# Conditioning vectors of layer 1 made on VectorE in the feed-forward of layer 0 instead of on TensorE in the mixer of layer 1

## The chip, the cores and the metric

The kernel runs on one core of a Trainium2 chip. The metric is device microseconds of one execution; the time of a kernel is the median of several. All times in the text are microseconds (us) unless marked ns. TensorE is PE in the rows (PEld: its weight loads), VectorE is DVE, ScalarE is ACT, and SP is the engine that issues the DMAs.

## The reference, cut to what matters

A batch of one sequence with 256 tokens of width 1024 goes through a first block of two layers and a second block of two layers, all in float32. The change lies in the first block alone. There every layer takes six vectors of width 1024 from one conditioning vector c:

```
ada = silu(c) @ w_ada[l] + b_ada[l]          # 1024 -> 6 * 1024
sh1, sc1, gt1, sh2, sc2, gt2 = split(ada)    # segments 0 .. 5
u = x * (1 + sc1) + sh1                      # mixer: attention, convolution, gates, w_out -> y
x = layer_norm(alpha * x + (1 + gt1) * y)
u = x * (1 + sc2) + sh2
x = layer_norm(alpha * x + (1 + gt2) * (relu(u @ w_up) ** 2 @ w_down))
```

A segment is a product of one row with a matrix of 1024 x 1024: 4 MB of weights are read for 1024 numbers. Segments 0, 1, 3 and 4 are wanted as columns (one number per partition), the gates 2 and 5 as a row on all partitions.

## The kernel before, in words

The weights stream from DRAM once. `weight_order` lists their pieces (1 MB each) in the order of use. `fetch` loads a piece into a `raw` buffer (3 of them), ScalarE casts it to a high part `whi` and VectorE subtracts to get the low part `wlo` (4 buffers each; lines L138 and L139, two halves of 1024 columns each). A product is three TensorE passes (high x high, high x low, low x high): `ws` with the weights stationary (L160, L161, L164), `as_` with the activations stationary (L180 to L182).

TensorE runs its instructions in the order of the program. VectorE, ScalarE and SP get an order from a planner, which goes by the order of the program and by times of its own model; on the chip every engine then keeps the order it was given. Between a product and the next one stands `handover` (residual, norm, feature-major operand), whose order on TensorE, VectorE and ScalarE is written out by hand.

Side work is a generator that `track` and `tick` advance: `track(gen, steps, us)` spreads so many steps over so many us of the main stream, and `ws_pair`, `branch` and the loop of `ffn1` call `tick` with what they take. So the place of a side step in the program, and with it the place of its TensorE instructions, is set by its number.

Conditioning has two forms. On VectorE, `ada_work` takes segments as 8 items of 128 rows or columns each. Item n loads a tile of 512 KB into one of two `ada` buffers (L354; the load of item n+1 is written before the work of item n, so it takes the buffer of item n-1), and VectorE then does one pass over 128x1024: for columns a product with `c_row` and a sum (L343), for a gate a multiply-add into an accumulator `acc` (L365 for its first item, L367 for the others). Six steps after the last item of a gate follow four steps `ada_gate`: one TensorE matmul with ones (L387) that sums a quarter of `acc` over the partitions, and two VectorE operations (L388, L390). On TensorE, `ada_pe` takes a segment as four pieces of 256 columns: two loads of 512 KB (L402), eight products in four column groups (L408), a ScalarE copy (L411), and then either `ada_gate` or two products of one column each (L418) and one VectorE operation (L421).

Before the change the mixer of layer 0 makes (0,4), (0,3), (0,2) on TensorE, the feed-forward of layer 0 makes (0,5), (1,1), (1,0) on VectorE, the mixer of layer 1 makes (1,3), (1,4), (1,2) on TensorE, and the feed-forward of layer 1 makes (1,5) on VectorE. `ffn1` is a loop over c = 2 .. 18: a `ws_pair` of w_up piece c, then `Out.add` of w_down piece c-3, about 11.2 us of TensorE together, with `tick` amounting to 10.4; at c = 15 what is left of the side work is written out. Beside it runs `rel_bias`, whose last instructions are a small table written to DRAM (L571) and a DMA of 1.5 MB from DRAM to DRAM (`toep<-rv`, L573).

In the mixer VectorE also does the depthwise convolution (`conv`, L909 and L912), which `conv_ln` transposes on TensorE (L927) before the branches that use it.

Of the kernel before, what the change touches and what calls it, by code (L numbers as in the profile page):

```python
# [28 lines left out]
def _two_pi():  # L29
    """2 pi as a sum of three floats, the first two with few digits."""  # L30
    c1 = 6.28125
    c2 = np.array([2 * math.pi - c1], np.float32)
    c2 = float((c2.view(np.uint32) & np.uint32(0xFFFFF000)).view(np.float32)[0])
    return c1, c2, float(np.float32(2 * math.pi - c1 - c2))
# [4 lines left out]
# columns of the packed per-partition parameters, and of the shape constants  # L39
# [21 lines left out]
PARTS = ((0, 512), (512, 768), (768, 1024))  # of the columns at the end of a product of 1024  # L61
ADA_PE = [(0, 4), (0, 3), (0, 2), (1, 3), (1, 4), (1, 2)]


class Net:
# [36 lines left out]
    def track(self, gen, steps, us):  # L102
        """Advance gen by `steps` steps over the next `us` of the main stream."""
        t = [gen, steps / us, 0.0]
        self.tracks.append(t)
        return t
# [17 lines left out]
    def fetch(self, parts=1):  # L124
        """One packed piece of a weight: its float32 values as hi + lo, both float32r."""
        nc = self.nc
        src = self.queue.pop(0)
        cols = src.shape[-1]
        raw = self.t("raw", [P, 2048])
        for a in range(0, cols, cols // parts):  # L130
            nc.sync.dma_start(raw[:, a:a + cols // parts], src[:, a:a + cols // parts])
        hi = self.t("whi", [P, 2048], F32R)
        lo = self.t("wlo", [P, 2048], F32R)
        step = cols // 2 if cols >= 1024 else cols
        with self.later():
            for a in range(0, cols, step):
                b = a + step
                nc.scalar.copy(hi[:, a:b], raw[:, a:b])  # L138
                nc.vector.tensor_sub(lo[:, a:b], raw[:, a:b], hi[:, a:b].bitcast(F32))  # L139
        self.ready.append((hi, lo))  # L140

    def w(self, ahead=2):
        """The next piece in weight_order; the pieces after it are already on their way."""
        while self.queue and len(self.ready) < 1 + ahead:
            self.fetch()
        return self.ready.pop(0)

    def split(self, hi, lo, src):
        """src (float32) as hi + lo."""
        a = self.nc.scalar.copy(hi, src)  # L150
        return a, self.nc.vector.tensor_sub(lo, src, hi.bitcast(F32))  # L151

    def ws(self, ps, w, blk, a, ks):
        """ps[cols of the weight, tokens] = W[:, cols]^T a   (weights stationary)."""
# [11 lines left out]
    def ws_pair(self, a, w=None):  # L166
        """Two column tiles (8 k tiles each) of the next weight piece -> psum [128, 2 x 256]."""
        w = w or self.w()
        p = self.ps()
        for m in range(2):  # L170
            self.ws(p[:, m * S:(m + 1) * S], w, m * 8, a, range(8))
            self.tick(2.6)
        return p

    def as_(self, ps, w, cols, a, k, h, first, last, **grp):
        """ps[tokens of half h, cols] += a^T W   (activations stationary)."""
# [7 lines left out]
    def as_512(self, a, first=False):  # L184
        """512 columns, two pieces of four k tiles -> psum of both halves.  first: another step before the
        last products of the first half."""
# [20 lines left out]
    class Out:  # L207
        """Product with 1024 columns, pieces of two k tiles: four accumulators; the last two pieces half by
        half, in PARTS of the columns."""

# [30 lines left out]
    def rstd(self, v, w):  # L241
        """v (> 0, [128, w]) -> v ** -0.5: a guess from the exponent, two refinements."""
# [29 lines left out]
    def rstd1(self, v, mul, eps, fill=()):  # L272
        """v ([128, 1]) -> (v * mul + eps) ** -0.5; the steps of rstd, their constants gathered into one
        factor that goes into v.  fill: work for VectorE in between."""
# [18 lines left out]
    def moments(self, st, eps, fill=()):  # L293
        """st: bn_stats of the pieces of a row -> mean, rstd."""
# [4 lines left out]
    def to_fm(self, src, n, evac):  # L299
        """src: [128 tokens, n * 128] in SBUF; evac(k0, nk, psum [128, nk, 128])."""  # L300
# [15 lines left out]
    def row(self, ap, n=D, pool="b4"):  # L316
        """A row of DRAM on all partitions."""
# [12 lines left out]
    def ada_cols(self, l, seg):  # L330
        """A shift (seg 0, 3) or 1 + scale (1, 4) as columns [128, 8]."""
# [8 lines left out]
    def ada_dot(self, l, seg, k, w):  # L340
        """One tile of columns: w [128 columns, 1024]; c_row is twice SiLU(c)."""
# [4 lines left out]
    def ada_work(self, segs):  # L346
        """On VectorE."""
# [32 lines left out]
    def ada_gate(self, l, seg, n, part, bb):  # L380
        """256 columns of a gate on all partitions: part summed over the partitions, + bias, + 1."""
# [10 lines left out]
    def ada_pe(self, segs):  # L392
        """On TensorE: 256 columns at a time, four k tiles side by side in the array."""
# [30 lines left out]
    def probs(self, q, k, bias):  # L424
        """q, k: [K, 256] feature-major (q scaled); bias [128, 256].  Unnormalised softmax numerators
        e [128, 384] (block 0: 128 keys | block 1: 256 keys) and the reciprocal row sums [128, 2]."""
# [18 lines left out]
    def p_t(self, e):  # L445
        """e [128 queries, 384] -> [128 keys, 384]: keys 0 x 256 queries | keys 1 x queries of block 1."""
# [8 lines left out]
    def attend(self, qk, v, bias, y):  # L455
        """qk(h) -> q, k; v(h, j) -> [128 keys, 64]; y feature-major [128, 4, 256].  Each step: the scores of
        one head, the transposed probabilities of the one before, the output of the pair before that."""
# [32 lines left out]
    def start(self):  # L490
        """Conditioning of the first mixer tile by tile, and with each tile its share of q, k, v and the
        first two pairs of the convolution's gated input."""
# [59 lines left out]
    def rel_bias(self):  # L552
        """DRAM [head, query in block, 256]: additive bias at distance 128 + p - j, -1e30 where masked."""
# [22 lines left out]
    def rope_tables(self):  # L576
        """cos, sin of positions * inv_freq for both halves: cc = [cos | cos], ss = [-sin | sin]."""
# [32 lines left out]
    def rope_tm(self, x, cc, ss):  # L610
        """In place: x [128, heads, 2, n]; cc, ss [128, 2, n]."""
# [11 lines left out]
    def handover(self, out, ch, nxt=None):  # L623
        """out: a product, its last pieces still to come; ch: the chain of a norm on it; nxt(u): generator of
        the first product behind.  Each engine in the order given here; -> what nxt yields."""
# [36 lines left out]
    def later(self):  # L662
        """What is traced here issues behind the last handover."""
        st = ExitStack()
        for ins in self.behind:
            st.enter_context(self.tc.issue_after(ins))
        return st

    class Norm:
        """x <- LN(ALPHA x + G acc) g + b;  u <- x A + B.   rms: x <- x + 0.5 acc;  u <- RMS norm of x times g.  # L670
        y: the rows before A, B (g)."""
# [12 lines left out]
        def transposed(self, h):  # L684
            """The row tiles k = 0, 1, 4, 5 in one bank, 2, 3, 6, 7 in another."""
# [93 lines left out]
    class RMSNorm(Norm):  # L779
        """ln: x is the layer norm of ALPHA x + G acc first."""  # L780
# [135 lines left out]
    def conv_ln(self, l, cv, hc):  # L916
        """LN over the channels, SiLU."""
# [32 lines left out]
    def mixer1(self, l, u, ps):  # L950
# [21 lines left out]
        if first:  # L972
# [4 lines left out]
            ada = self.track(self.ada_pe(ADA_PE[:3]), 25, 62)  # L977
# [6 lines left out]
        else:  # L984
            keep(2, ps)
            ada = self.track(self.ada_pe(ADA_PE[3:]), 25, 80)
# [68 lines left out]
        self.finish(ada)  # L1055
# [13 lines left out]
    def ffn1(self, l, u, ps):  # L1069
        nc = self.nc  # L1070
        segs = [(0, 5), (1, 1), (1, 0)] if l == 0 else [(1, 5)]
# [56 lines left out]
    def fm_512(self, u, scale):  # L1128
        """512 columns feature-major [128, 4, 256], one piece (256 columns) per step."""
# [12 lines left out]
    def mla_norm(self, pcs, gq, n_):  # L1142
        """RMS norms of the low-rank q and kv; feature-major."""
# [23 lines left out]
    def mixer2(self, l, u, ps):  # L1167
        nc, i = self.nc, self.i
        gq = self.row(i["mla_g"][l])
        # low-rank q and kv, and the rotary key: token-major  # L1170
# [31 lines left out]
        # q of C: 64 + 32 + zeros per head  # L1202
# [18 lines left out]
        # k, v of C  # L1221
# [59 lines left out]
        # gates, then the branches  # L1281
# [33 lines left out]
    def diff(self, l, li, lam, qb, kb, vb, y):  # L1315
        """Differential attention of B, its RMS norm; y feature-major."""
# [105 lines left out]
def weight_order(i):  # L1422
    """The packed pieces of the weights in the order of their use."""
# [48 lines left out]
def _tiles(w, order, per=16):  # L1472
    """w [K, N] -> [chunks, 128, per * 128]: the 128 x 128 tiles (k, n) in the given order."""
# [18 lines left out]
def _fm(v):  # L1492
    """[..., n * 128] -> [128, ... * n]"""
# [123 lines left out]
```

## Time and profile before

| What | us |
|---|---|
| median of 3 runs | 1746.57 (1746.49 to 1747.38) |
| span of the profiled execution, first to last instruction | 1744.7 |
| median less span: what lies around the span | 1.9 |
| feed-forward of layer 0, TensorE between the handovers | about 229 to 400 |
| mixer of layer 1, first product to the next handover | about 420 to 578 |
| TensorE busy over the span | 1693.0 (97%) |

The profile is one execution. Times in its rows count from the first instruction. The own time of the profiled execution is not given beside its span; the median of the runs stands for it, 1.9 us above the span.

### The profile page before, as it was taken

The numbers are of one execution on the slowest core, as the hardware profiler recorded it, in microseconds if no ns is written. First come the engines' busy times: TensorE is split into PE (matmuls) and PEld (weight loads), VectorE is DVE, ScalarE is ACT, GpSimd is POOL, SyncE is SP. The second block draws the span as 40 slices with busy tenths as digits, with TensorE's granted clock in tenths as the row PEclk, the third lists the DMA queues.
The fourth block names the chain that finished last, engine by engine and source line by source line (L and its number), as shares of the span: only waits on it lengthen the run. The fifth ranks groups of instructions, "written<-read, shape, count | busy, mean of one in ns | idle before, by whom it ended". The sixth has DMA issues, their size and how long they took to land.

```text
span 1744.7 us, 28878 instructions
## 1 busy us (share of the span) xinstructions
PE 1693.0 (97%) x11736; PEld 1533.6 (88%) x11736; DVE 1203.8 (69%) x2281; ACT 894.8 (51%) x1550; POOL 2.6 (0%) x12
## 2 busy tenths in 40 slices
PE   6998999999999999988999999999999999999998
PEld 5887888888889899977998898999989889989997
DVE  7999887478997785468555667655675555875554
ACT  3664464355355455435566645444455666454442
POOL 0000000000000000000000000000000000000000
PEclk9999999999999999998999999999999999999999
DMA  9885568495865286635643344655454444446551
GB/s 339 339 309 188 190 228 332 168 341 187 300 233 206 97 320 217 205 130 207 209 140 130 138 156 137 239 190 191 151 210 161 147 145 145 163 158 209 183 184 47
DMA packets 59986, 347.58 MB, mean 199 GB/s; under 512 B 6558, under 2 KB 10700, under 8 KB 25676
## 3 DMA queue, kind: packets, MB, share of 16 engines
q1 hardware_dynamic: 59852, 345.73, 55.8%
q8 instruction: 92, 1.51, 0.3%
q14 instruction: 42, 0.34, 0.1%
HBM read 344.63 MB, written 2.64 MB: 199 GB/s over the span
## 4 chain that ended last, share of the span: by engine, by line
PE 89%; DVE 7%; ACT 2%; issue 1%; DMA 1%; SPq 0%; ACTq 0%; DVEq 0%
PE ps L160 16%; PE ps L161 16%; PE ps L164 16%; PE ps L181 8%; PE ps L180 8%; PE ps L182 7%; PE ps L196 3%; PE ps L202 3%; PE ps L197 3%; PE ps L430 1%; PE ps L450 1%; DVE wlo L139 1%; PE ps L306 1%; PE ps L429 1%; PE ps L408 1%
## 5 line engine op out<-in xcount | busy, mean ns | idle before, releaser
L139 DVE TENSOR_TENSOR wlo<-raw,whi 128x1024 fp32r<-128x1024 f32 (+1 forms) x534 | 630.4, 1212 | 306.1 <-ACT whi L138 304.2
L138 ACT CAST whi<-raw 128x1024 fp32r<-128x1024 f32 (+1 forms) x534 | 532.3, 1042 | 431.6 <-PE ps L161 186.2
L160 PE MATMUL ps<-s,whi 128*128 128x256 f32 x2400 | 602.6, 288 | 0.2 <-DVE s L901 0.2
L161 PE MATMUL ps<-s,whi 128*128 128x256 f32 x2400 | 590.5, 283 | 0.0
L160 PEld LDWEIGHTS ps<-s,whi 128*128 128x128 f32 x2400 | 459.8, 192 | 20.2 <-issue 16.1
L161 PEld LDWEIGHTS ps<-s,whi 128*128 128x128 f32 x2400 | 460.9, 192 | 2.4
L164 PE MATMUL ps<-s,wlo 128*128 128x256 f32 x2400 | 343.8, 284 | 1.3 <-DVE wlo L139 1.3
L164 PEld LDWEIGHTS ps<-s,wlo 128*128 128x128 f32 x2400 | 312.9, 192 | 1.5 <-DVE wlo L139 1.5
L180 PE MATMUL ps<-whi,s 128*128 128x512 f32 (+2 forms) x736 | 273.5, 372 | 12.8 <-ACT s L150 11.7
L181 PE MATMUL ps<-wlo,s 128*128 128x512 f32 (+2 forms) x736 | 273.1, 371 | 1.4 <-DVE wlo L139 1.4
L182 PE MATMUL ps<-whi,s 128*128 128x512 f32 (+2 forms) x736 | 271.8, 369 | 0.0
L180 PEld LDWEIGHTS ps<-whi,s 128*128 128x128 f32 x736 | 139.9, 190 | 34.7 <-ACT s L150 11.7
L181 PEld LDWEIGHTS ps<-wlo,s 128*128 128x128 f32 x736 | 139.9, 190 | 22.9 <-DVE wlo L139 2.5
L182 PEld LDWEIGHTS ps<-whi,s 128*128 128x128 f32 x736 | 139.6, 190 | 22.5
L196 PE MATMUL ps<-whi,s 128*128 128x512 f32 x240 | 97.9, 408 | 3.5 <-ACT s L761 3.5
L912 DVE SCALAR_TENSOR_TENSOR s<-s,dw,s 128x255 f32<-128x255 f32 (+14 forms) x240 | 96.8, 463 | 0.0
L197 PE MATMUL ps<-wlo,s 128*128 128x512 f32 x240 | 94.9, 396 | 0.0
L151 DVE TENSOR_TENSOR s<-ev,s 128x256 fp32r<-128x256 f32 (+1 forms) x72 | 39.1, 543 | 72.7 <-PE ps L181 54.0
L150 ACT CAST s<-ev 128x256 fp32r<-128x256 f32 (+1 forms) x72 | 36.1, 501 | 75.9 <-DVE ev L1392 73.5
L202 PE MATMUL ps<-whi,s 128*128 128x512 f32 x240 | 66.0, 398 | 0.0
L196 PEld LDWEIGHTS ps<-whi,s 128*128 128x128 f32 x240 | 45.8, 191 | 17.0 <-ACT s L761 5.4
L197 PEld LDWEIGHTS ps<-wlo,s 128*128 128x128 f32 x240 | 45.9, 191 | 9.1
(235 smaller groups left out, 1365.7 us busy)
## 6 DMA issues: line engine op xcount, KB each, us to landing
raw<-in_w_fgu_dram SPq DMA_DIRECT2D x44, 1024.0 KB, 4.9
raw<-in_w_up_dram SPq DMA_DIRECT2D x32, 1024.0 KB, 5.8
raw<-in_w_down_dram SPq DMA_DIRECT2D x32, 1024.0 KB, 5.1
raw<-in_w_in_dram SPq DMA_DIRECT2D x32, 1024.0 KB, 4.9
ada<-in_w_ada_p_dram SPq DMA_DIRECT2D x48, 512.0 KB, 4.6
raw<-in_w_gate_dram SPq DMA_DIRECT2D x24, 1024.0 KB, 4.8
raw<-in_w_fd_dram SPq DMA_DIRECT2D x22, 1024.0 KB, 4.8
raw<-in_w_in_b_dram SPq DMA_DIRECT2D x18, 1024.0 KB, 7.1
```

Of the source, the lines that this page charges most:

```text
L138: nc.scalar.copy(hi[:, a:b], raw[:, a:b])
L139: nc.vector.tensor_sub(lo[:, a:b], raw[:, a:b], hi[:, a:b].bitcast(F32))
L160: mm(ps, whi[:, b], ahi[:, k, :], start=j == 0, stop=False)
L161: mm(ps, whi[:, b], alo[:, k, :], start=False, stop=False)
L164: mm(ps, wlo[:, b], ahi[:, k, :], start=False, stop=j == n - 1)
L180: mm(ps, ahi[:, k, tok], whi[:, cols], start=first, stop=False, **grp)
L181: mm(ps, ahi[:, k, tok], wlo[:, cols], start=False, stop=False, **grp)
L182: mm(ps, alo[:, k, tok], whi[:, cols], start=False, stop=last, **grp)
L196: mm(p, ahi[:, k, tok], whi[:, cols], start=k == 0, stop=False)
L197: mm(p, ahi[:, k, tok], wlo[:, cols], start=False, stop=False)
L202: mm(p, alo[:, k, tok], whi[:, cols], start=False, stop=k == 7)
L912: nc.vector.scalar_tensor_tensor(cv[:, ct, d:], hp[:, ct, :S - d], wk, cv[:, ct, d:], op0=ALU.mult, op1=ALU.add)
```

## The change

`ADA_PE` keeps only the three segments of layer 0. The mixer of layer 1 runs no `ada_pe` any more. In `ffn1` of layer 0 `ada_work` gets six segments instead of three, 48 items instead of 24, with (1,2), (1,4), (1,3) behind the three of before; its track becomes 54 steps over 160 us instead of 30 over 160. The host packs fewer tiles into `w_ada_p`. The other lines of the diff take out comments.

```diff
-ADA_PE = [(0, 4), (0, 3), (0, 2), (1, 3), (1, 4), (1, 2)]
+ADA_PE = [(0, 4), (0, 3), (0, 2)]
...
-            ada = self.track(self.ada_pe(ADA_PE[:3]), 25, 62)
+            ada = self.track(self.ada_pe(ADA_PE), 25, 62)
...
             keep(2, ps)
-            ada = self.track(self.ada_pe(ADA_PE[3:]), 25, 80)
+            ada = None
...
-        self.finish(ada)
+        if ada:
+            self.finish(ada)
...
     def ffn1(self, l, u, ps):
-        segs = [(0, 5), (1, 1), (1, 0)] if l == 0 else [(1, 5)]
+        segs = [(0, 5), (1, 1), (1, 0), (1, 2), (1, 4), (1, 3)] if l == 0 else [(1, 5)]
         ada = self.track(self.ada_work(segs), 8 * len(segs) + 6, 160 if l == 0 else 80)
```

## Rows read from the trace of the kernel before

**Rows 1.** Page, part 1: busy us (share of span) x instructions.
```profile
PE 1693.0 (97%) x11736; PEld 1533.6 (88%) x11736; DVE 1203.8 (69%) x2281; ACT 894.8 (51%) x1550; POOL 2.6 (0%) x12
```

**Rows 2.** Chain of work in the mixer of layer 1: start us, us, engine, tile, line.
```profile
424.15 0.96 PE ps L164 x8
...
427.03 0.96 PE ps L164 x8
427.99 1.00 PE ps L408 x16
...
431.09 0.96 PE ps L164 x8
434.40 0.96 PE ps L164 x8
...
507.11 0.43 PE ps L387 x2
...
539.62 1.02 PE ps L927 x8
```

**Rows 3.** Stretches: length; busy PE, PEld, DVE, ACT, POOL; PEclk; DMA share; GB/s.
```profile
230.00:393.00 163.00, 161.70 (x1027) 146.47 (x1026) 115.39 (x132) 84.76 (x106) 0.00 (x0) 1.00 0.79 287
320.00:340.00 20.00, 20.00 (x122) 17.94 (x121) 2.68 (x7) 7.49 (x10) 0.00 (x0) 1.00 0.04 15
420.00:526.40 106.40, 106.40 (x834) 90.08 (x833) 100.27 (x226) 53.35 (x99) 0.00 (x0) 1.00 0.76 276
```

**Rows 4.** VectorE instructions in order of time, feed-forward of layer 0: the items.
```profile
239.57 0.75 DVE L365 TENSOR_SCALAR b<-ada,c_col 128x1024 f32<-128x1024 f32 x1
...
305.02 1.28 DVE L343 CUSTOM_DVE_ANT_0 ada<-ada,c_row,par 128x1024 f32<-128x1024 f32 x1
...
339.35 0.69 DVE L151 TENSOR_TENSOR s<-ev,s 128x512 fp32r<-128x512 f32 x1 [7.43 <-PE ps L181]
...
340.62 1.28 DVE L343 CUSTOM_DVE_ANT_0 ada<-ada,c_row,par 128x1024 f32<-128x1024 f32 x1
...
370.89 1.28 DVE L343 CUSTOM_DVE_ANT_0 ada<-ada,c_row,par 128x1024 f32<-128x1024 f32 x1
```

**Rows 5.** SP, waits of the DMA queue from 220 to 400: us, times, longest.
```profile
SPq L354 <- DVE ada L343: 59.2, 12, 28.8
SPq L354 <- DVE b L367: 17.2, 7, 3.7
```

**Rows 6.** DMA issues from 220 to 400 (median landing), then landing minimum, median, maximum.
```profile
ada<-in_w_ada_t_dram SPq DMA_DIRECT2D x16, 512.0 KB, 6.5
```
```profile
DMA to landing us min/median/max: 3.7/6.2/14.0
```

**Rows 7.** SP in order of time around the table DMA.
```profile
301.93 0.88 SPq L573 DMA_DIRECT2D toep<-rv  x1
302.93 4.40 SPq L354 DMA_DIRECT2D ada<-in_w_ada_t_dram  x1
...
309.31 0.33 SPq L354 DMA_DIRECT2D ada<-in_w_ada_t_dram  x1
```

**Rows 8.** TensorE in order of time: first gate matmul; first product of c = 14.
```profile
318.46 0.59 PE L387 MATMUL ps<-b,ones 128*128 128x256 f32 x2
```
```profile
363.73 0.28 PE L160 MATMUL ps<-s,whi 128*128 128x256 f32 x1
```

**Rows 9.** VectorE in order of time: last convolution step, first handover operation of layer 0.
```profile
525.52 0.81 DVE L912 SCALAR_TENSOR_TENSOR s<-s,dw,s 128x226 f32<-128x226 f32 x2
```
```profile
395.17 0.68 DVE L721 TENSOR_TENSOR ev<-ps,G 128x512 f32<-128x512 f32 x1
```

**Rows 10.** Stretches around TensorE's stand in the mixer of layer 0, columns as in 3.
```profile
152.00:154.00 2.00, 1.24 (x5) 1.06 (x6) 2.00 (x4) 0.00 (x0) 0.00 (x0) 0.50 0.00 0
154.00:156.00 2.00, 2.00 (x12) 2.00 (x11) 2.00 (x5) 0.00 (x0) 0.00 (x0) 0.50 0.03 8
156.00:158.00 2.00, 2.00 (x13) 1.95 (x13) 2.00 (x7) 0.00 (x0) 0.00 (x0) 0.75 0.47 66
```

## Prediction

> **What bounds the kernel now.** The page's first part comes first: TensorE is busy 97% of the span [rows 1], so work taken off it should count in full wherever nothing else comes to the fore. Next the two stages that the change touches, as stretches [rows 3]: in both TensorE is the only engine without idle time, but VectorE is close behind, 115.4 us of 163 in the feed-forward of layer 0, and 100.3 of 106.4 in the mixer of layer 1 up to the end of its convolution. So the mixer has little room under TensorE. Then the items in the feed-forward, in order of time [rows 4], and what their loads wait for [rows 5]: SP waits 76 us for VectorE to give an `ada` buffer back. That stream is held by its two buffers.
>
> **What is removed.** In the chain [rows 2] two halves of a `ws_pair` start 2.88 us apart (424.15, 427.03); with eight L408 products between them it is 4.06 (427.03 to 431.09), with L418 between them 3.31 (431.09 to 434.40). A piece of `ada_pe` thus costs TensorE 1.18 + 0.43 us; a gate's piece has L387 in place of L418, also 0.43. Twelve pieces are 12 x 1.61 = 19.3 us, all but one L387 ahead of the transposes L927 at 539.62 [rows 2], which would come 18.9 us earlier, at 520.7. They need the convolution, which VectorE ends at 526.3 [rows 9]. VectorE has 106.4 - 100.27 = 6.1 us idle up to there [rows 3]: with all of it gone the convolution ends at 520.2, as now at 526.3. So TensorE would wait at L927 between 0 and 5.6 us, or longer if work that stands behind 526 now (weights and softmax that the faster TensorE wants sooner) moves in ahead; I take 4. The mixer of layer 0 has such a wait: TensorE stands, and when it is back at 152.8 its granted clock is 0.50, the lower of its two levels (1.2 GHz), until about 157 [rows 10]; that costs 1.24 x 0.5 + 1 + 0.5 = 2.1 us. With 2 for this the mixer gives 19.3 - 4 - 2 = 13.3 us, with bounds of 10 and 19. The 24 loads of 512 KB that leave it, and the ScalarE copies, were hidden under TensorE and give nothing.
>
> **What is added to the feed-forward of layer 0.** Four gate matmuls, 4 x 0.43 = 1.7 us of TensorE. On VectorE 24 passes of at most 1.28 us [rows 4], 30.7 us, and eight small gate operations; VectorE has 163 - 115.4 = 47.6 us free [rows 3], so by the sum it fits. The 24 loads are 12.6 MB, which over 163 us add 77 GB/s to the 287 of the stretch [rows 3]; I give that no term of its own, since the two buffers hold the loads back first. The sums hide the order, and there I see the cost.
>
> The gate (1,2) is items 24 to 31. Its matmuls stand in TensorE's order at step n + 2 = 39 with n = 37 (six after item 31). The rule for the place: with 30 steps in 160 us the gate (0,5) comes at step 15, tick 80, and (80 - 5.2)/10.4 = 7.19 loops, which is the middle of the pair of c = 10; there it is, at 318.46 [rows 8]. With 54 steps, step 39 is tick 115.6, 10.61 loops, the end of c = 13. TensorE now passes that place at 363.73 [rows 8]. TensorE keeps its order, so if item 31 is not done by then, all products behind wait for it.
>
> When is item 31 done? Item 0 starts at 239.57, item 15 at 305.02 [rows 4]: 4.36 us each. Items 16 to 23 go from 340.62 to 370.89: 4.32 each. That is what two buffers allow: a load waits for the item two before, lands after 6.5 us in the median of this stage [rows 6], and the item takes 1.28; (6.5 + 1.28)/2 = 3.9, and some waits. Writing the items closer together in the program doesn't make this faster, since SP already waits for buffers. So at 305 the stream would again be near item 15.
>
> Between 305 and 340.62 there is a pause. The table DMA is issued at 301.93 [rows 7], and the two items whose loads come behind it stand in VectorE's order after L151 of c = 11 at 339.35, which waits for TensorE [rows 4]; the weights issued behind it are as late, and for 20 us the DMA engines are almost empty [rows 3]. My reading is that the planner expects that DMA to hold up the loads behind it much longer than it does. The table stays where it is, so I expect the pause again, with item 16 near 340.6. By 363.73 item 21 has started (340.62 + 5 x 4.32 = 362.2). Ten more are wanted. While TensorE stands, the weights' loads soon stop for want of buffers, and an item's load can land as fast as the quickest here, 3.7 us [rows 6]: (3.7 + 1.28)/2 = 2.5 us each. Item 31 then starts at 387.2 and ends at 388.5: TensorE waits 24.8 us, and 2.1 more go to its clock. Bounds: 43 us if the loads get no faster (340.62 + 15 x 4.32 + 1.3 = 406.7), 15 if the stream is three or four items further at the pause.
>
> Last, items 32 to 47. From 388.5 TensorE has the 31.4 us of before (363.73 to the first handover operation, 395.17 [rows 9]) and at 4.32 us seven of them go by; nine remain for the handover, whose chain runs over VectorE, or for the mixer. Nothing here shows which: from 0 to 9 x 1.28 = 11.5 us, and I take 4, somewhat under the middle, since the handover has some idle VectorE time.
>
> **The Trainium skill, weighed.** The rows say 6.5 us from issue to landing of 512 KB in this stage and 3.7 at best [rows 6]. The Trainium skill ("DMA: Bandwidth & Descriptors", section "Anatomy of one DMA") gives a fit, for transfers issued by gpsimd: about 2.0 us fixed plus the bytes over 436 GB/s. As an estimate from that page, 512 KB take 3.2 us and the stream could run at (3.2 + 1.28)/2 = 2.2 us per item, so TensorE would never wait. The trace agrees with it only for the quickest load; with weights under way beside it, it does not.
>
> **Sum for the likeliest case (A).** 24.8 + 2.1 + 1.7 + 4 - 13.3 = +19.3 us. The span is 1744.7 and the median 1.9 above it, so 1746.6 + 19.3 = 1765.9, forecast 1766. A's own range is 1752 to 1783.
>
> **The rivals.** B: the pause does not come back, the pace stays 4.36. Item 28 starts at 361.6, three more at 2.5 us, item 31 is done at 370.4: a wait of 6.7. Sum 6.7 + 2.1 + 1.7 + 4 - 13.3 = +1.2, 1748; 1741 to 1754. For it: the pause is the planner's doing, and its order is made anew. Against it: weights and items alike were late behind the table.
>
> C, the other side: the stream keeps ahead of TensorE. It must do an item in (363.73 - 1.28 - 239.57)/31 = 3.96 us without pause; the place is the `ada` buffers, the price nothing but the matmuls. Then 1.7 - 13.3 = -11.6, or with the mixer's full 19 us -17.3: 1735, from 1729 to 1741. For it: 3.9 from landing and item time; more items nearer in the program get precedence over weights. Against it: 76 us of waiting for buffers, and the pause. The skill's fit would give this case.
>
> D: A, and the leftover items sit in the mixer, where VectorE is 94% busy, so the convolution ends 11 us later and most of the mixer's gain is lost: 1783 to 1797.
>
> **Chances.** A 0.55, B 0.18, C 0.22, D 0.05. A measurement of this kernel tells about 0.2%, 3.5 us, from no change: faster is under 1743.1, slower over 1750.1. Faster: C and 0.05 of B, 0.27. Same: most of B and the edge of A, 0.11. Slower: 0.62. The range from 1731 to 1782 leaves out D, the top of A and the bottom of C.
>
> **What the profile after would show.** A: TensorE idle ahead of L387 between c = 13 and 14, ended by L367; a lower granted clock behind; item 16 near 340; loads near 4 us during the stand. B: the same wait, some 7 us, with items through 305 to 340. C: no TensorE wait there, items under 4 us apart. In the mixer TensorE some 19 us shorter, with a wait at L927 for L912. I am wrong if the items run faster than two buffers let them before, or if the planner moves the table.

## The result, and the profile after

The changed kernel takes 1762.0 us (1760.7 to 1767.65, 4 runs), the kernel before on the same chip 1747.0: a ratio of 1.009, 95% interval 1.0071 to 1.0108. The forecast was 1766, slower; the sign and the size held, the mechanism did not. The profiled execution took 1760.7, the shortest of the four; its span is 1758.9.

TensorE's part of the page against [rows 1], then the first VectorE operation of the handover behind the feed-forward of layer 0 and of the one behind the mixer of layer 1, first in the changed kernel:

```profile
PE 1687.2 (96%) x11512; PEld 1531.0 (87%) x11512; DVE 1229.1 (70%) x2313; ACT 891.2 (51%) x1538; POOL 2.6 (0%) x12
```
```profile
420.53 0.69 DVE L721 TENSOR_TENSOR ev<-ps,G 128x512 f32<-128x512 f32 x1 [1.24 <-PE ps L182]
...
599.26 0.69 DVE L721 TENSOR_TENSOR ev<-ps,G 128x512 f32<-128x512 f32 x1
```

Before, the two stood at 395.17 [rows 9] and 585.11. From handover to handover the feed-forward of layer 0 went from 190.3 to 215.1 us (+24.8), the mixer of layer 1 from 189.9 to 178.7 (-11.2); all later stages are as long as they were. These two lengths are what the experiments below are read by. Each comes from the one profiled execution of its kernel, while the medians come from all of them.

Where the 24.8 us lie: the same stretch from handover to handover, first before, then after (columns as in [rows 3]).

```profile
204.90:395.20 190.30, 186.29 (x1166) 167.32 (x1166) 138.66 (x186) 98.81 (x130) 0.00 (x0) 1.00 0.70 254
```
```profile
205.40:420.50 215.10, 196.37 (x1167) 172.69 (x1167) 165.12 (x232) 96.47 (x128) 0.00 (x0) 0.96 0.77 273
```

TensorE's idle time rose from 4.0 to 18.7 us, and its busy time by 10.1. Of this the matmuls of the added gate are 1.7, at the price of 0.43 forecast for each of four. Most of the other 8.4 is the granted clock, 0.96 over the stretch instead of 1.00. It was 0.50 in these three parts of the stage (columns as before):

```profile
331.94:338.77 6.83, 5.99 (x28) 5.99 (x29) 4.57 (x4) 1.74 (x2) 0.00 (x0) 0.50 0.87 302
345.59:352.42 6.83, 5.88 (x14) 4.63 (x15) 5.50 (x5) 2.05 (x3) 0.00 (x0) 0.50 0.85 279
417.27:420.53 3.26, 1.25 (x4) 1.06 (x5) 2.03 (x4) 1.45 (x2) 0.00 (x0) 0.50 1.00 418
```

TensorE is busy for 13.1 us in them, and at twice the clock that would be 6.6 less. The last 1.8 us of busy time are not accounted for. What TensorE waited for, 220 to 430 (us, times, longest):

```profile
PE ps L181 <- DVE wlo L139: 7.1, 8, 2.6
PE ps L180 <- ACT whi L138: 5.3, 3, 2.0
PE ps L160 <- ACT whi L138: 3.6, 1, 3.6
```

It waited for weights, which stand in no step of the prediction. The gate matmul L387, at which the prediction put the wait, has none: its 16 instances in this stage have no idle time before them. The items did what they needed for that: item 31 starts at 359.90, and TensorE comes to its gate at 380.12. Item 0, the item before the pause, the two rows at the end of the pause, and item 47, in VectorE's order:

```profile
238.15 0.75 DVE L365 TENSOR_SCALAR b<-ada,c_col 128x1024 f32<-128x1024 f32 x1
...
316.62 1.28 DVE L343 CUSTOM_DVE_ANT_0 ada<-ada,c_row,par 128x1024 f32<-128x1024 f32 x1 [1.54 <-DMA ada<-in_w_ada_t_dram]
...
329.11 0.69 DVE L151 TENSOR_TENSOR s<-ev,s 128x512 fp32r<-128x512 f32 x1 [6.05 <-PE ps L181]
329.72 1.28 DVE L343 CUSTOM_DVE_ANT_0 ada<-ada,c_row,par 128x1024 f32<-128x1024 f32 x1
...
416.80 1.28 DVE L343 CUSTOM_DVE_ANT_0 ada<-ada,c_row,par 128x1024 f32<-128x1024 f32 x1
```

That is 178.65 us for 47 items, 3.80 each, with a pause of 13 us (316.62 to 329.72) where [rows 4] has 35. None of the 48 is left for the handover.

The price is seen in SP's queue. First the changed kernel, then before, nearly the same place (start us, us, line, transfer, count; a count of 2 starts within the time given):

```profile
292.66 2.93 SPq L354 DMA_DIRECT2D ada<-in_w_ada_t_dram  x2
295.68 0.38 SPq L131 DMA_DIRECT2D raw<-in_w_down_dram  x1
300.03 2.94 SPq L354 DMA_DIRECT2D ada<-in_w_ada_t_dram  x2
303.07 0.37 SPq L131 DMA_DIRECT2D raw<-in_w_up_dram  x1
```
```profile
277.96 0.33 SPq L354 DMA_DIRECT2D ada<-in_w_ada_t_dram  x1
279.10 0.33 SPq L131 DMA_DIRECT2D raw<-in_w_down_dram  x1
282.32 0.33 SPq L354 DMA_DIRECT2D ada<-in_w_ada_t_dram  x1
284.59 0.33 SPq L131 DMA_DIRECT2D raw<-in_w_up_dram  x1
```

The planner now writes two item loads ahead of each piece of weights, where it wrote one. TensorE uses up a piece in 5.61 us (11.22 per loop of two, as from c = 13 at 352.51 to c = 14 at 363.73 before). Before, pieces were issued every 5.15 us (ten steps from 261.36 to 312.83); now every 6.82 (seven steps from 261.55 to 309.26), so that the lead of the weights shrinks by 1.2 us with each. Then comes the table:

```profile
312.36 0.87 SPq L573 DMA_DIRECT2D toep<-rv  x1
313.98 5.00 SPq L354 DMA_DIRECT2D ada<-in_w_ada_t_dram  x1
319.08 0.37 SPq L354 DMA_DIRECT2D ada<-in_w_ada_g_dram  x1
319.54 0.38 SPq L131 DMA_DIRECT2D raw<-in_w_up_dram  x1
331.03 1.19 SPq L354 DMA_DIRECT2D ada<-in_w_ada_g_dram  x2
332.32 0.38 SPq L131 DMA_DIRECT2D raw<-in_w_down_dram  x1
```

The piece issued at 319.54, behind the table, lands only some 12 us later. ScalarE has waited for it (start us, us; in brackets the wait and what ended it), and TensorE's longest wait, the 3.6 us at L160 above, is for this cast:

```profile
331.69 1.99 ACT L138 CAST whi<-raw 128x1024 fp32r<-128x1024 f32 x2 [5.98 <-DMA raw<-in_w_up_dram]
```

No piece is issued between 319.54 and 332.32. Before, the gap was longer still, 29.6 us (312.83 to 342.38), and TensorE did not notice [rows 3]: the lead covered it. Counted from 229 on, 18 pieces had been issued when that gap began. Now it is 15, and 6.7 us later, so that the lead at this point is smaller by some 23 us (3 x 5.61 + 6.7), while the gap is only 16.8 shorter. From there on the chain of work runs through the queue (start us, us, what):

```profile
329.72 1.30 DVE ada L343 x2
...
331.90 0.33 SPq L354
332.32 9.45 DMA raw<-in_w_down_dram
341.85 1.05 ACT whi L138
...
345.26 1.22 DVE wlo L139
346.48 1.21 DVE b L367
347.71 0.33 SPq L354
348.08 8.38 DMA raw<-in_w_down_dram
356.54 1.06 ACT whi L138
```

Read it as a ring: an item on VectorE gives its buffer back, SP can issue the item load that waited for it and only then the piece behind that load, the piece lands 8.4 to 9.5 us later, ScalarE and VectorE split it, and the next item stands behind that split in VectorE's order. After the pause a piece comes every 7.68 us (six steps from 332.32 to 378.38). Between 330 and 340 the granted clock is 0.66:

```profile
330.00:340.00 10.00, 7.21 (x38) 7.22 (x39) 6.77 (x8) 1.99 (x2) 0.00 (x0) 0.66 0.71 252
```

### The profile page after: what moved, and what is told of

The parts are those of the page before. It is cut to its first block, busy times and chain, and to the rows that moved or that the text cites. A ratio compares the mean times of both kernels' runs of the same rounds, so it can differ in the third digit from the quotient of the medians.

```text
span 1758.9 us, 28445 instructions
## 1 busy us (share of the span) xinstructions
PE 1687.2 (96%) x11512; PEld 1531.0 (87%) x11512; DVE 1229.1 (70%) x2313; ACT 891.2 (51%) x1538; POOL 2.6 (0%) x12
## 4 chain that ended last, share of the span: by engine, by line
PE 83%; DVE 9%; DMA 4%; ACT 2%; issue 1%; SPq 0%; ACTq 0%; DVEq 0%
PE ps L160 16%; PE ps L161 15%; PE ps L164 15%; PE ps L181 7%; PE ps L182 7%; PE ps L180 7%; PE ps L196 3%; PE ps L202 3%; PE ps L197 3%; DMA raw<-in_w_down_dram 2%; DVE wlo L139 2%; PE ps L430 1%; PE ps L450 1%; DMA raw<-in_w_in_a_dram 1%; PE ps L306 1%
## 5 line engine op out<-in xcount | busy, mean ns | idle before, releaser
L160 PE MATMUL ps<-s,whi 128*128 128x256 f32 x2400 | 604.1, 289 | 3.8 <-ACT whi L138 3.6
L160 PEld LDWEIGHTS ps<-s,whi 128*128 128x128 f32 x2400 | 461.2, 192 | 23.0 <-issue 15.2
L180 PE MATMUL ps<-whi,s 128*128 128x512 f32 (+2 forms) x736 | 275.5, 374 | 18.2 <-ACT s L150 11.8
L151 DVE TENSOR_TENSOR s<-ev,s 128x256 fp32r<-128x256 f32 (+1 forms) x72 | 39.1, 543 | 56.1 <-PE ps L181 38.5
L196 PEld LDWEIGHTS ps<-whi,s 128*128 128x128 f32 x240 | 45.9, 191 | 15.5 <-ACT s L761 5.4
```

The costliest lines, as they stand in the source:

```text
L160: mm(ps, whi[:, b], ahi[:, k, :], start=j == 0, stop=False)
L180: mm(ps, ahi[:, k, tok], whi[:, cols], start=first, stop=False, **grp)
L196: mm(p, ahi[:, k, tok], whi[:, cols], start=k == 0, stop=False)
```

## The experiments

The first theory after the result was: the items' pace of 3.80 us, times the number of items that the planner puts ahead of a piece (54 steps / 160 us x 10.4 / 2 = 1.76), is 6.7 us for a piece, over 5.61. Its rivals were VectorE's load, the DMA's bytes, and something in the mixer. The ratios are to runs of the kernel before on the chip of the same experiment, where its median was 1746.95 to 1747.99. Lengths below are from handover to handover, as above; "ff" is the feed-forward of layer 0, "mixer" that of layer 1.

| kernel | median us | ratio to before, 95% | ff | mixer |
|---|---|---|---|---|
| before | 1747.0 | | 190.3 | 189.9 |
| changed | 1762.0 | 1.0071 to 1.0108 | 215.1 | 178.7 |
| mixer's part alone | 1733.45 | 0.990 to 0.993 | 190.3 | 174.5 |
| items alone | 1776.82 | 1.0146 to 1.0177 | 213.2 | 195.4 |
| items from GpSimd, changed | 1796.94 | 1.0253 to 1.0298 | 252.7 | 175.9 |
| items from GpSimd, before | 1753.65 | 1.0022 to 1.0043 | 194.0 | 190.0 |
| one segment moved | 1743.72 | 0.9971 to 0.9989 | 190.3 | 186.1 |
| two segments moved | 1758.08 | 1.0045 to 1.0078 | 204.7 | 184.6 |
| changed, no added passes | 1755.87 | 1.0032 to 1.0062 | 211.2 | 179.0 |
| changed, half tiles | 1764.12 | 1.0074 to 1.0110 | 217.0 | 181.4 |
| changed, half the bytes | 1748.69 | 0.9997 to 1.0016 | 200.5 | 180.3 |
| changed, table later | 1757.93 | 1.0035 to 1.0068 | 201.4 | 180.9 |
| two segments, table later | 1741.98 | 0.9961 to 0.9983 | 191.7 | 182.0 |
| before, table later | 1746.71 | 0.9982 to 1.0002 | 187.1 | 189.9 |

### The two parts of the change, each alone

The mixer's part: no `ada_pe` in the mixer of layer 1, and nothing added to the feed-forward. The three vectors are not made at all; GpSimd fills them with ones.

```diff
-        segs = [(0, 5), (1, 1), (1, 0), (1, 2), (1, 4), (1, 3)] if l == 0 else [(1, 5)]
+        segs = [(0, 5), (1, 1), (1, 0)] if l == 0 else [(1, 5)]
+        if l == 0:
+            self.ada[1, 2] = self.t("G", [P, D], tag="G2")
+            nc.gpsimd.memset(self.ada[1, 2], 1.0)
+            for s in (4, 3):
+                nc.gpsimd.memset(self.ada_cols(1, s), 1.0)
```

> Only what the change takes out: the mixer of layer 1 without its vectors, and no items added to the feed-forward of layer 0; the three vectors are filled with ones, so the products that make them are left out. Theory (parts add up): the mixer's stage, 189.9 us before and 178.7 after the change, is near 179, the feed-forward stays at 190, the whole is 1734 to 1738. Rival, the mixer gained because its weights and VectorE's work were further ahead after the late feed-forward: less than 8 us gained, over 1739. If all 19.3 us of TensorE count: 1727.

Measured: 1733.45; the mixer 15.5 us shorter (174.5, where 179 was expected), the feed-forward as before. The items' part: the kernel before with 48 items, its mixer left as it is.

```diff
-        segs = [(0, 5), (1, 1), (1, 0)] if l == 0 else [(1, 5)]
+        segs = [(0, 5), (1, 1), (1, 0), (1, 2), (1, 4), (1, 3)] if l == 0 else [(1, 5)]
```

> Only what the change puts in: the kernel before with the 24 added items in the feed-forward of layer 0, while the mixer of layer 1 makes the three vectors again on TensorE. Theory (parts add up): the feed-forward's stage near 215 us as after the change, the mixer's near 190, the whole 1768 to 1774 us. Rival, the cost depends on the loads of the mixer's tiles no longer standing ahead of the handover: the stage differs by more than 5 us from 215.

Measured: 1776.82, above the 1768 to 1774 expected; feed-forward +22.9, mixer +5.5. So the 24 items cost the feed-forward nearly what the whole change costs it (24.8), without the mixer's part, and its lateness runs on into the mixer: 5.5 us here, and in the changed kernel the mixer gained 11.2 instead of 15.5. The parts add up: 22.9 + 5.5 - 15.5 = 12.9 against 13.6 in the changed kernel.

### Is it SP's queue alone?

All item loads of the stage issued by GpSimd instead of SP, in the changed kernel and, as its control, in the kernel before.

```diff
-            nc.sync.dma_start(w, src)
+            (nc.gpsimd if segs[0][0] == 0 else nc.sync).dma_start(w, src)
```

> The changed kernel with the loads of all 48 items of the feed-forward of layer 0 issued by GpSimd, so that no weights stand behind them in SP's order. Bytes, buffers and VectorE's passes stay. Theory (the weights wait in SP's order behind two item loads, each of which waits for its buffer): the stage from handover to handover, 215.1 us after the change against 190.3 before, falls to 192 to 198 us, the whole to 1738 to 1745 us. Rival, the DMA engines' rate is what limits (57 MB in the stage): the bytes are the same, so the stage stays over 210 and the whole over 1757. Rival, VectorE's added 31 us: stays over 210 as well.

> The kernel before with its 24 items' loads issued by GpSimd: what the other queue does by itself. Theory: before the change SP had one item load per piece of weights and TensorE waited 1.3 us in the stage, so 1743 to 1749 us. If the queue by itself gives several us, the reading of the run above has to be corrected by it. If loads from GpSimd are slow, over 1752.

Measured: 1796.94 and 1753.65. The run doesn't settle what SP's queue costs, since the edit did more than it was meant to: with the loads out of SP the planner made VectorE's order anew, and put a run of 18 items ahead of one half of a `wlo`. TensorE stood for all of them (waits of TensorE from 206 to 470, then one stretch):

```profile
PE ps L164 <- DVE wlo L139: 43.6, 1, 43.6
```
```profile
370.00:400.00 30.00, 0.00 (x0) 0.00 (x0) 14.99 (x25) 0.00 (x0) 5.61 (x11) 0.50 0.61 187
```

What it shows is that an item can hold up a piece in VectorE's order as well as in SP's. In the kernel before, the same edit cost 3.7 us in the feed-forward, of 5.7 in all. The loads from GpSimd were not slow there, 5.3 us in the median against 6.5 [rows 6]; TensorE waited 3.1 us for one `wlo`.

### The number of items

One or two of the three segments moved, the others left on TensorE in the mixer.

```diff
-ADA_PE = [(0, 4), (0, 3), (0, 2)]
+ADA_PE = [(0, 4), (0, 3), (0, 2), (1, 3), (1, 2)]
...
-        segs = [(0, 5), (1, 1), (1, 0), (1, 2), (1, 4), (1, 3)] if l == 0 else [(1, 5)]
+        segs = [(0, 5), (1, 1), (1, 0), (1, 4)] if l == 0 else [(1, 5)]
```

> Only one of the three vectors, (1,4), is made in the feed-forward of layer 0 (32 items instead of 48 there); the other two, (1,3) and (1,2), stay on TensorE in layer 1's mixer. Theory (pace of the items): the planner's order gives 38 steps in 160 us of the feed-forward, 10.4 us of it for two pieces of weights, so 38/160*10.4/2 = 1.24 items for each piece; at 3.80 us per item a piece is met after 4.7 us, and TensorE asks for one every 5.62, so the weights are not late: feed-forward of layer 0 190 to 194 us, the mixer 4 to 6.4 shorter than 189.9, total 1740 to 1746. If each added item simply cost time (24.8 us / 24 items, a linear price for VectorE's or the DMA's work), 8 items would cost 8.3: feed-forward 198.6, total 1749 to 1752.

> Two of the three vectors, (1,4) and (1,3), are made in the feed-forward of layer 0 (40 items); (1,2) stays on TensorE in layer 1's mixer. Theory (pace of the items): 46 steps in 160 us give 1.50 items for each piece of weights; 1.50*3.80 = 5.7 us against the 5.62 that TensorE needs: just at the edge, feed-forward 191 to 200 us, mixer 7.5 to 13 shorter than 189.9, total 1736 to 1748. A linear price of 24.8/24 us per added item would give 190.3 + 16.5 = 206.8 for the feed-forward and a total near 1754.

Measured: with one segment the feed-forward is as long as before (190.3) and the kernel is faster than before, 1743.7; the linear price of 8.3 us is refuted. With two it is 204.7, some 5 us over the theory's 191 to 200: a threshold there is, but it lies lower than the pace alone gives. The trace of the kernel with two segments shows why: TensorE waits first behind the table's gap (309.84 to 332.15 without a piece), and then, from 350 to 400, it is nearly full (49.4 of 50 us) although 40 items run beside it.

```profile
330.00:340.00 10.00, 6.26 (x38) 5.86 (x36) 6.51 (x10) 0.00 (x0) 0.00 (x0) 0.83 0.77 269
340.00:350.00 10.00, 7.63 (x21) 5.70 (x22) 7.25 (x10) 5.73 (x7) 0.00 (x0) 0.66 0.76 252
...
360.00:370.00 10.00, 10.00 (x68) 9.26 (x67) 8.60 (x10) 4.43 (x6) 0.00 (x0) 1.00 0.87 319
```

### VectorE's passes, the buffers, the bytes

Three cuts into an item. First without the arithmetic of the added items; a copy of one column stands for the pass in 23 of the 24:

```diff
+            if l == 1 and seg in (3, 4):
+                nc.vector.tensor_copy(self.ada_cols(l, seg)[:, k:k + 1], w[:, 0:1])
+            elif l == 1 and seg == 2 and k > 0:
+                nc.vector.tensor_copy(acc[:, k:k + 1], w[:, 0:1])
...
```

> The changed kernel, without the VectorE arithmetic of its 24 added items: each still loads its 512 KB tile and gives its buffer back after a copy of one column, so the three vectors have wrong values. Theory (pace of the items): an item then holds its buffer for the landing alone, so the mean pace falls from 3.80 to between 2.5 and 3.3 us, 1.76 items per piece are met in 4.4 to 5.8 us, and the feed-forward of layer 0 is 190 to 197 us instead of 215.1; total 1735 to 1742. If it is VectorE's work as such that delays the weights, the same times come out, so this run does not tell these two apart. If the bytes (57 MB in this stretch, unchanged) set the end, the stage stays at 210 or more and the total above 1755.

Then with each item's tile in two halves and four half buffers in place of the two; the tiles of `ada_pe` are halved with them, and one row moves to another buffer:

```diff
-            w = self.t("ada", [P, 1024])
...
-            nc.sync.dma_start(w, src)
...
+            for lo, hi in HALVES:
+                w = self.t("adah", [P, 512])
+                nc.sync.dma_start(w, src[:, lo:hi])
...
```

> The changed kernel with each item's 512 KB tile loaded as two tiles of 256 KB, in four buffers of half the size (the same space, bytes and VectorE elements; one more fixed cost of a pass for each item). Theory (pace of the items): a half can be loaded while the other half of the same buffer space is being worked on, so an item's pace falls from 3.80 to 2.8 to 3.3 us, 1.76 items per piece are met in 4.9 to 5.8 us: feed-forward of layer 0 191 to 199 us, total 1738 to 1747. If VectorE's load or the bytes set the end, nothing is gained (VectorE has rather more to do): stage 212 to 220, total 1759 to 1768.

Measured: 211.2 and 217.0, where the theory wanted 190 to 199. The theory as it stood, that the two buffers set the pace and the pace sets the end, fell. Both lengths, and the totals of 1755.9 and 1764.1, lie where the expectations put them if the bytes set the end. So VectorE's load is not the main cause either: without the passes VectorE was busy 23.8 us less in the stage (141.4 instead of 165.1), and the stage is 3.9 us shorter. Stretch 330 to 400 of the changed kernel, of the one without passes, and of the one with half tiles:

```profile
330.00:400.00 70.00, 60.09 (x344) 52.80 (x345) 50.75 (x65) 27.05 (x32) 0.00 (x0) 0.90 0.84 295
```
```profile
330.00:400.00 70.00, 62.30 (x364) 53.20 (x365) 32.33 (x59) 30.25 (x37) 0.00 (x0) 0.95 0.89 321
```
```profile
330.00:400.00 70.00, 63.66 (x369) 55.08 (x369) 54.39 (x96) 28.92 (x34) 0.00 (x0) 0.93 0.87 309
```

Two items and a piece are 2.1 MB; for one such group in 5.61 us the DMA would have to bring 374 GB/s. It brought 295, and 309 to 321 with the buffers relieved, its engines 84 to 89% busy in all three. That is not the most it can bring: in the kernel before it was 422 between 270 and 280. A piece came every 6.49 us without the passes (eight steps from 332.62 to 384.56) and every 6.75 with half tiles (nine from 329.97 to 390.74): sooner than 7.68, still later than TensorE wants it. In this run, where two to four halves stand one behind the other, a load of half the size landed no sooner (issues from 206 to 425, median to landing; half tiles, then the changed kernel):

```profile
adah<-in_w_ada_t_dram SPq DMA_DIRECT2D x64, 256.0 KB, 4.8
```
```profile
ada<-in_w_ada_t_dram SPq DMA_DIRECT2D x32, 512.0 KB, 4.7
```

Third, the added items with half the bytes and the full VectorE work, two passes over the half that is loaded:

```diff
+            if l == 1 and seg in (2, 3, 4):
+                nc.sync.dma_start(w[:, :512], src[:, :512])
...
```

> The changed kernel, where each of the 24 added items loads only the first half of its tile (256 KB) and VectorE passes over that half twice, so VectorE's elements, the items and their order stay and only the bytes of the added items are halved (the three vectors have wrong values). Theory (bytes): without VectorE's passes the stream still needed 6.4 us for two items and one piece of weights, 2.1 MB, that is 328 GB/s; with halves the same group is 1.57 MB, 4.8 us, under the 5.62 that TensorE takes for a piece, so the weights keep their lead: feed-forward of layer 0 190 to 197 us, total 1737 to 1745. Rival (order and buffers: weights stand in the queue behind item loads that wait for one of two buffers): in the run with half tiles a 256 KB load landed after 4.8 us, no sooner than one of 512 KB in the changed kernel (4.7), so the hold of a buffer is hardly shorter and the feed-forward stays at 205 us or more, total above 1750.

Measured: 200.5, and 1748.7 in all, between the two. The expectation had overlooked that the 24 items of before come first and keep their full size, so that up to the table nothing is changed (a piece every 6.9 us). Behind the table the halves rule, and there a piece comes every 4.8 us (six steps from 332.57 to 361.46) and TensorE is full again:

```profile
340.00:400.00 60.00, 59.62 (x361) 53.11 (x360) 56.61 (x97) 33.76 (x41) 0.00 (x0) 1.00 0.87 317
```

That agrees with the bytes, but it doesn't isolate them, since the planner's order changed too: there 1.5 items stand ahead of a piece, not two.

### The gap behind the table

`rel_bias`, with the table's DMA, made in the feed-forward of layer 1; in the changed kernel, with two segments, and in the kernel before.

```diff
-        rel = self.track(self.rel_bias(), 5, 60) if l == 0 else None
+        rel = self.track(self.rel_bias(), 5, 60) if l == 1 else None
```

> The changed kernel with the bias table of the second block (its four small loads, its matmuls and the 1.5 MB table) made in the feed-forward of layer 1 instead of layer 0. In all runs so far the queue stood for 11 to 24 us behind the table, with no piece of weights issued. If that pause is the whole cause, TensorE never starves: feed-forward of layer 0 190 to 195 us, total 1737 to 1743. If bytes and pause share it, the stage is what 57.4 less 1.6 MB take at 328 GB/s, 170 us from 228 on, so an end some 400 us into the run and a stage of 195 to 205 us, total 1742 to 1751. If the pause was harmless (weights late by their pace alone), 212 to 216, total above 1757.

> Two of the three vectors, (1,4) and (1,3), in the feed-forward of layer 0, (1,2) on TensorE in layer 1's mixer, and the bias table in the feed-forward of layer 1. 1.5 items for each piece are 1.84 MB, 5.6 us at 328 GB/s, just what TensorE takes for a piece. If the pause behind the table is what made the 40 items late (204.7 us), the feed-forward of layer 0 falls to 190 to 196 us and the total from 1758.1 to 1743 to 1750; if not, 202 us or more and 1755 or more.

> The kernel before with the bias table made in the feed-forward of layer 1 instead of layer 0, as in the two runs with a late table. Theory: before, 24 items leave the weights their lead (one item for each piece), so the pause behind the table cost TensorE nothing there: feed-forward of layer 0 stays at 190 to 192 us, and the move only adds the 1.7 us that it cost in the feed-forward of layer 1 in those two runs: total 1746 to 1751. Rival (the pause costs about 13 us whatever the items, and before had it hidden elsewhere in the sum): feed-forward 178 to 185 us, total under 1742.

Measured, in the profiled executions: the feed-forward falls from 215.1 to 201.4 and, with two segments, from 204.7 to 191.7 (190 to 196 expected); in the kernel before only from 190.3 to 187.1 (3.2 us where none was expected; 1.7 of them come back in the feed-forward of layer 1, 188.9 instead of 187.2, with the table's matmuls). So in these executions the gap costs the kernel before next to nothing and the others some 10 us more. Without it the price of the items is +4.6 for 16 (191.7 against 187.1) and +14.3 for 24 (201.4); with it, +14.4 and +24.8.

The medians bear this out for two segments (1758.1 to 1742.0, 16.1 us) but not in full for the changed kernel. Its run with the table later took 1751.6 to 1759.1 in five executions, and the profiled one is the shortest of them, 6.3 under the median. By the median the table's move gives it 4.1 us (1762.0 to 1757.9), or some 7 by the two ratios (1.009 and 1.005). That median lies in the range that the expectation gave for a harmless gap (above 1757), while the profiled stage of 201.4 lies in that for bytes and gap together (195 to 205). With 24 items the share of the gap stays open between these; the stage was not profiled in the longer executions.

TensorE around the place where the gap was, in the changed kernel and with two segments, table later:

```profile
320.00:340.00 20.00, 17.73 (x111) 15.59 (x110) 14.10 (x16) 6.93 (x9) 0.00 (x0) 1.00 0.84 291
```
```profile
320.00:340.00 20.00, 20.00 (x126) 18.08 (x125) 13.89 (x19) 8.77 (x11) 0.00 (x0) 1.00 0.80 311
```

Two segments with the table later is 1742.0, ratio 0.9961 to 0.9983; with one segment and the table where it was 1743.7, 0.9971 to 0.9989. Both beat the kernel before and the changed one; between themselves they can't be told apart.

### What stays open

How the 2.07 us by which a piece comes late (7.68 against 5.61) divide between bytes and buffers: relieving the buffers took 0.9 to 1.2 of it, yet hardly moved the stage's end. That the rest is the bytes is argued from the 295 to 321 GB/s, and not shown; why the DMA brought no more there, when it brought 422 in another stretch, is open too. An order of SP and VectorE with the weights always first, at the same bytes, was not tried, since the planner makes both orders.

## Why the prediction was right in size and wrong in mechanism

**Right in size: the mixer's gain.** Twelve pieces were to give 19.3 us of TensorE; its busy time in the mixer fell by 18.2 in the run of that part alone. The stage gained 15.5 there, 11.2 in the changed kernel, against 13.3 forecast with bounds of 10 and 19. The wait was named at L927 for the convolution (4 us); there is none. TensorE came to L927 14 us sooner after its handover and found the convolution just done; it waited 2.2 us in two parts one step later, for the norm behind it (waits of the changed kernel, 420 to 600):

```profile
PE ps L692 <- DVE x L738: 3.5, 2, 3.0
PE ps L181 <- DVE wlo L139: 2.6, 1, 2.6
PE ps L306 <- DVE ev L932: 2.2, 2, 1.4
```

The first row was 1.6 before, the second, weights late again, was not there. With the granted clock between 420 and 460, 0.95, they stand behind the 4.3 us that the mixer loses here against the run of its part alone (178.7 and 174.5): TensorE is idle 2.0 us more and busy 2.3 us more. No lower clock followed the wait of 2.2, for which 2 us had been set down.

**Wrong: the pace of the items, 4.32 to 4.36.** It was taken as the most that two buffers allow. With 54 steps the same two buffers gave 3.80, pause included, and 3.57 up to the pause; what set the pace before is not shown. Items 0 to 31 took 3.93 each, so the condition of case C (3.96) was met, and items 24 to 31 were done before TensorE came to L387. The 76 us of SP waiting for buffers [rows 5] showed that SP had time to spare, not that the stream could go no faster.

**Wrong: the pause.** It was forecast as before, 35 us with item 16 at 340.6. The table's DMA came 10 us later (312.36 against [rows 7]), and the pause was 13 us. The item behind it stood once more behind an L151 that waited for TensorE, as read from [rows 4]. But its harm was looked for in the items, which had time, and not in the pieces of weights in the same queue.

**The step that failed: "I give that no term of its own, since the two buffers hold the loads back first".** That sentence dealt with the 24 added loads as so many GB/s. Two things were not asked: in what order the added loads stand in SP's queue against the pieces that TensorE waits for, and how much lead the pieces have. The rows were there: 29.6 us without a piece and TensorE full [rows 3] meant a lead that I estimate at 24 us or more (29.6 - 5.6), which one item load per piece kept up and two per piece would use up. Case C even names the order, "more items nearer in the program get precedence over weights", as a point for the items and without a price for the weights. What the runs showed in its place: a piece every 6.82 us and later every 7.68 instead of 5.15, and 16.0 us of TensorE waiting for weights.

**Right by chance: the sum.** 24.8 us of waiting at L387 were forecast, and the stage grew by 24.8; but those are 14.7 more of idle TensorE, most of it waits for weights, and 10.1 of busy time, mostly at a lower clock and in the gate's matmuls. The whole forecast for the stage was 32.6 (24.8 + 2.1 + 1.7 + 4), 7.8 too much, and the mixer's gain was 2.1 too high (13.3 against 11.2), which took back a part of that. The clock was mis-sized, 2.1 forecast and about 6.6 measured, since TensorE stood many times and not once. The 4 us for leftover items in the handover were 0. Case C was wrong in its price only: it had the stream ahead of TensorE at "nothing but the matmuls". The column items' loads did come sooner than before, 4.7 us in the median against 6.5 (the gates' hardly, 5.7 against 5.8), while the weights took longer, 8.1 and 7.2 against 6.3 and 5.8. The estimate by the Trainium skill ("DMA: Bandwidth & Descriptors", section "Anatomy of one DMA"), 3.2 us for 512 KB, agrees with neither median of the column items; and it speaks of one transfer, issued by GpSimd, while what decided here was what stood behind a load in SP's queue.

## What to carry to other kernels

Side loads that share a queue with the main stream are not free when their engine has time: count how many stand ahead of each main load, and compare the time of that group with what the consumer takes for one. Look for how much lead the main stream has, and for every place where it is spent (here the gap behind the table), because moved work can be free up to that lead and dear beyond it: 8 added items cost the stage nothing, 16 cost it 14 us, and taking the table out of the way gave the whole kernel about 1 us before the change, 16 with two segments moved, and 4 to 7 with all three. Where the work can be moved in parts, move the part that fits, and take other things out of the crowded stage.

## What the runs showed of the hardware that was not expected

- Beside weights loads, 256 KB landed after 4.8 us in the median and 512 KB after 4.7, where the halves of an item were issued one behind the other. Where one half was loaded alone (half the bytes, 325 to 410), 256 KB of a column item landed after 3.7 us, against 4.3 for 512 KB in the changed kernel in the same stretch.
- The DMA held 295 to 321 GB/s over 70 us with two item loads and one of 1 MB in turn, at 84 to 89% of its engines' time. In short stretches it was more: 406 with several loads of 1 MB queued (two segments moved, 400 to 410), and 422 in the kernel before (270 to 280).
- In the run with 43.6 us without a TensorE product the granted clock was 0.50 from 370 to 400, where TensorE stood, and still 0.50 between 400 and 410, where it took up work again. In the changed kernel waits of at most 3.6 us went with 0.66 to 0.88 in three stretches of 10 us (330 to 360), and in the whole stage the clock cost not quite half of what the added idle time did (6.6 us beside 14.7).
